# Summing the conditioning over partitions by TensorE transposes and ScalarE accumulating copies in a fused FP32 hybrid layer

## The chip, the cores and the metric

One Trainium2 chip, one core of it. The metric is the device time of the kernel in microseconds (us); the times given are medians over repeated runs. A trace of one profiled execution stands beside them. Engines are named as the trace names them: PE is TensorE's matmul, PEld its weight load, DVE is VectorE, ACT is ScalarE, POOL is GpSimd, SP is the queue that issues the DMAs.

## The reference, cut to what matters

```python
cond = jax.nn.silu(c)                                # (1, 2048)
mod = cond @ w_mod[l] + b_mod[l]                     # w_mod: (2048, 6*2048)
sh1, sc1, gt1, sh2, sc2, gt2 = jnp.split(mod, 6, axis=-1)
u = rms_norm(h, norm1_g[l]) * (1.0 + sc1) + sh1      # h: (1, 256, 2048)
aq, ak, av, rq, rf, ri, rg, ga, gr = split_columns(u @ w_in[l])
...
h = h + gt1 * (merged @ w_o[l])
u = rms_norm(h, norm2_g[l]) * (1.0 + sc2) + sh2
ffn = (jax.nn.silu(u @ w_ffn_gate[l]) * (u @ w_ffn_up[l])) @ w_ffn_down[l]
h = h + gt2 * ffn
return rms_norm(h, final_g)
```

All of it is FP32; the sequence has 256 rows, the model width is 2048. The conditioning vector `mod` decides shift (`sh`) and scale (`sc`) of both norms, so no product with `w_in` can start before the shift and scale of its rows of `u` are known.

## The kernel before, in words

**Products.** Every weight tile `w` (four k-blocks of 128 rows by 512 columns, one DMA) is cast by ACT to a rounded high part `wh` (L240), and DVE forms the low part `wl` = `w` - `wh` (L242), two k-blocks per instruction. `products` (L245) then issues three matmuls per k-block and half of the sequence: `wh` with `uH` (L250), `wl` with `uH` (L251) and `wh` with `uL` (L252), all into one accumulator `acc` per half. `wh` and `wl` live in pools of four buffers each: a fifth cast waits until PE has finished with the oldest.

**Chunks.** The columns of `w_in` for the first seven outputs are worked in 14 column groups, and the k-blocks in four chunks (3, 4, 5 and 4 blocks, `chunk_cols` and `group`): all 14 groups of chunk 0, then all 14 of chunk 1, and so on, the sums kept in SBUF tiles `part`. Between chunks 0 and 1 PE goes from products with rows 0 to 2 of `uH`, `uL` straight to products with rows 3 to 6.

**Conditioning.** `mod_cols` computes shift and scale of some k-blocks. DVE accumulates `cond`-weighted rows of `w_mod` tiles `wm` into two tiles `modc` (one for shift, one for scale; L403 starts, L407 adds), where each partition holds the sum over its own rows. What is left is a sum over the 128 partitions, and a change of layout: the result must have one column per k-block, channels on partitions. `col_sum` (L333) does both by one FP32 matmul per 128 columns with a column of ones as the moving operand: its output is a [128, 1] column of the PSUM tile `pmc`. DVE then adds the bias (L426, L427) and forms `(1 + sc) * g` (L428). For the first norm `modulated` (L378) follows for every k-block: ACT computes `u` = `xT` times scale plus shift (L373) and its high part `uH` (L383), DVE the low part `uL` (L384).

**Order of the work.** `mod_cols` is a generator. While chunk `ci` runs, `step` advances the one of chunk `ci + 1` after each weight tile; `chunk_cols` sets the pace so that it is through shortly before the chunk ends (`AHEAD` = 1.15), and `drain` runs what is left. `GAP1`, the number of steps between sums and their use, is 0 here. Three later calls (L-numbers of the profile: sums at 749, 854 and 916 us) make the second norm's conditioning while `w_o` and the first FFN tiles are worked: 16, 8 and 8 column sums. Beside those, chunk 0 has 6 sums, chunk 1 has 8, chunk 2 has 10 and chunk 3 has 8. A scheduler then puts the instructions of all engines into queues, one per engine, each of which the engine works strictly in order.

Of the kernel before, what the change touches and what calls it, by code (L numbers as in the profile page):

```python
# [8 lines left out]
F32 = mybir.dt.float32  # L9
# [3 lines left out]
AF = mybir.ActivationFunctionType  # L13
# [5 lines left out]
P = 128  # L19
D = 2048  # L20
S = 256
KT = D // P
# [29 lines left out]
def block_kernel(  # L52
# [7 lines left out]
    nc = tc.nc  # L60
    x, out = x[0], out[0]
# [4 lines left out]
    small = ctx.enter_context(tc.tile_pool(name="small", bufs=4))  # L66
# [11 lines left out]
    def bank(name):  # L78
        return ps.tile([P, 512], F32, tag="ps", name=name)

    def tmpt(name, n=512, dt=F32):
        return tmp.tile([P, n], dt, tag=f"t{n}", name=name, bufs={512: NT, 256: 2}[n])
# [7 lines left out]
    ident = const.tile([P, P], F32, name="ident")  # L90
# [137 lines left out]
    def load_mod(k0, nk, n0, ncol, own):  # L228

        if own:  # L230
            dst = wpool.tile([P, nk, ncol], F32, tag="wm", name="wm", bufs=NM)
        else:
            dst = bigt("wm0")[:, :nk * ncol].rearrange("p (k n) -> p k n", n=ncol)
        return load(w_mod, k0, nk, n0, ncol, dst)
# [98 lines left out]
    def col_sum(p, j0, a, n):  # L333
        for j in range(n):
            mm(p[:, j0 + j:j0 + j + 1], a[:, j * P:(j + 1) * P], ones[:, 0:1], start=True, stop=True)  # L335
# [4 lines left out]
    junk = const.tile([P, NG], F32, name="junk")  # L340
# [37 lines left out]
    def modulated(src, k, H, L):  # L378

        u = tmpt("u", S)  # L380
        scale_shift(UACT, u, src, k)
        h = H(k, slice(0, S))
        nc.scalar.copy(out=h, in_=u)  # L383
        nc.vector.tensor_sub(out=L(k, slice(0, S)), in0=u, in1=h.bitcast(F32))  # L384

    def mod_loads(nk):
        wid = nk * P
        kk = min(KT, 1024 // wid)
        return [(q, min(kk, KT - q)) for q in range(0, KT, kk)]

    def mod_cols(k0, nk, chunk, gcol, src, H, L, after=None, room=0, lag=0):

        wid = nk * P
        a = [tmp.tile([P, 1024], F32, tag="modc", name=f"modc{ci}", bufs=2) for ci in range(2)]
        waiting = []

        def sums(q, kk, ci, w):
            for j in range(kk):  # L400
                s1, d = cond[:, q + j:q + j + 1], a[ci][:, :wid]
                if q + j == 0:
                    first = nc.vector.tensor_scalar_mul(out=d, in0=w[:, j], scalar1=s1)  # L403
                    if after is not None:
                        tc.add_manual_dep(first.ins, after.ins.name, NOSYNC, reason="the norm goes first")
                else:
                    nc.vector.scalar_tensor_tensor(out=d, in0=w[:, j], scalar=s1, in1=d, op0=ALU.mult, op1=ALU.add)  # L407

        for q, kk in mod_loads(nk):
            for ci in range(2):  # L410
                waiting.append((q, kk, ci, load_mod(q, kk, (chunk + ci) * D + k0 * P, wid, q >= room)))
                if ci == 0:
                    yield
            while len(waiting) > (lag if q < room else 0):
                sums(*waiting.pop(0))
            yield
        for w in waiting:
            sums(*w)
        p = bank("pmc")
        for ci in range(2):  # L420
            col_sum(p, ci * nk, a[ci], nk)
        for _ in range(GAP if chunk else GAP1):
            yield
        ks = slice(k0, k0 + nk)
        bc = [bcols[:, (chunk + ci) * KT + k0:(chunk + ci) * KT + k0 + nk] for ci in range(2)]
        nc.vector.tensor_add(out=sh_col[:, ks], in0=p[:, 0:nk], in1=bc[0])  # L426
        nc.vector.tensor_add(out=sc_col[:, ks], in0=p[:, nk:2 * nk], in1=bc[1])  # L427
        nc.vector.scalar_tensor_tensor(out=sc_col[:, ks], in0=sc_col[:, ks], scalar=1.0, in1=gcol[:, ks], op0=ALU.add, op1=ALU.mult)  # L428
        if src is not None:
            for k in range(k0, k0 + nk):  # L430
                modulated(src(k, slice(0, S)), k, H, L)
# [31 lines left out]
    def mods1(ci):  # L463
        k0, nk = kchunks[ci]
        return mod_cols(k0, nk, 0, g1c, xTv, uH, uL, room=(KT, KT // 2, 0, 0)[ci], lag=(0, 4, 0, 0)[ci])
# [253 lines left out]

    cond_side.append(mod_rows("gt1", 2))  # L720
    cond_side.append(mod_cols(0, KA, 3, g2c, None, None, None))
    pace["cond"] = PACE2
    side.append(attention(0))
# [117 lines left out]
    for k0, nk in KREST:  # L841
        cond_side.append(mod_cols(k0, nk, 3, g2c, x2Tv, u2H, u2L, last_norm2[-1] if PIN else None))
        pace["cond"] += AHEAD * 2 * len(mod_loads(nk)) / nsteps
# [14 lines left out]
    for part_n, ng in enumerate((6, 5)):  # L858
        fH, fL = [None] * ng, [None] * ng
        for g in range(ng):  # L860
# [3 lines left out]
            for t in range(2):  # L864
                if early:
                    a = fpart[2 * g][:, t]
                    nc.vector.tensor_add(out=a, in0=pg[t], in1=a)
                    nc.scalar.activation(a, a, AF.Silu)
                else:
                    a = tmpt("sl")  # L870
# [62 lines left out]
```

## Time and profile before

| | |
|---|---|
| median of 3 runs | 1547.67 us (1547.43 to 1552.2) |
| profiled execution, its own time | 1543.71 us |
| its span in the trace | 1541.5 us |
| granted clock | 0.998 |
| busy: PE, DVE, ACT | 97%, 71%, 48% |
| chain of waits: PE, DVE, DMA, ACT | 89%, 5%, 3%, 2% |

"Busy" is the share of the span in which an engine had an instruction under way; a matmul's duration overlaps the next one's, so start-to-start distances, not durations, tell what a matmul costs. The chain of waits goes back from the last instruction, at each step to what released it. A row of the timeline has the start, the duration, the engine, the line, output <- inputs, shapes and count, and in brackets how long the engine had been idle and who ended it.

### The profile page before, as it was taken

Reading aid. Unit: us, or ns where it says so; the run is one execution under the profiler, and the core shown is the slowest. Engines: PE = TensorE matmul, PEld = TensorE weight load, DVE = VectorE, ACT = ScalarE, POOL = GpSimd, SP = SyncE. Lnnn points to the kernel's source line nnn. Section 1 sums busy time; section 2 is a strip of 40 time slices with the busy share of each in tenths; the row PEclk is TensorE's granted clock in tenths of the full one; section 3 lists DMA queues with packets and bytes.
Section 4 is the critical chain, followed back from the end, with each engine's and each line's share of the span. In section 5 each row is a group of like instructions: output and inputs, shape, how many; then the busy total and the mean of one; then the engine's idle time right before and its main releaser. Section 6 shows DMA issues by size and latency. Waiting matters only on the chain.

```text
span 1541.5 us, 18297 instructions
## 1 busy us (share of the span) xinstructions
PE 1495.4 (97%) x6931; PEld 1233.7 (80%) x6931; DVE 1101.4 (71%) x1439; ACT 732.4 (48%) x1015; POOL 10.5 (1%) x40
## 2 busy tenths in 40 slices
PE   3999999999999999999989999999999999999997
PEld 2788888888878778888878888888888888888885
DVE  5789997788877688987578778879555555544555
ACT  5563433524567764444464554444333444444443
POOL 1000000000000000000000000000000000000000
PEclk9999999999999999999999999999999999999999
DMA  9899998444764389899549988868555655556552
GB/s 312 306 327 320 314 322 273 165 137 150 253 239 150 110 306 337 319 333 333 194 156 352 329 316 286 296 222 304 199 196 196 196 180 191 187 187 219 190 194 103
DMA packets 175987, 373.67 MB, mean 242 GB/s; under 512 B 8430, under 2 KB 12695, under 8 KB 175899
## 3 DMA queue, kind: packets, MB, share of 16 engines
q1 hardware_dynamic: 174776, 371.77, 69.9%
q8 instruction: 54, 0.88, 0.2%
q10 hardware_dynamic: 1122, 0.74, 0.2%
q14 instruction: 35, 0.28, 0.0%
HBM read 370.38 MB, written 2.10 MB: 242 GB/s over the span
## 4 chain that ended last, share of the span: by engine, by line
PE 89%; DVE 5%; DMA 3%; ACT 2%; issue 1%; SPq 0%; DVEq 0%; ACTq 0%
PE acc L250 27%; PE acc L251 27%; PE acc L252 27%; PE ptr L504 2%; DMA wm<-in_w_mod_dram 2%; DVE wl L242 2%; PE pl L589 2%; DVE modc L407 1%; PE pmc L335 1%; DMA w<-in_w_in_dram 1%; ACT junk L343 1%; PE psc L652 0%; PE prow L330 0%; PE pav L683 0%; DMA rows<-in_gnorm_g_dram 0%
## 5 line engine op out<-in xcount | busy, mean ns | idle before, releaser
L240 ACT CAST wh<-w 128x1024 fp32r<-128x1024 f32 (+1 forms) x518 | 529.7, 1030 | 673.9 <-PE acc L252 575.5
L242 DVE TENSOR_TENSOR wl<-w,wh 128x1024 fp32r<-128x1024 f32 (+1 forms) x518 | 613.9, 1193 | 324.3 <-ACT wh L240 323.1
L250 PE MATMUL acc<-wh,uH 128*128 128x512 f32 x704 | 277.7, 394 | 2.4 <-ACT uH L383 2.4
L251 PE MATMUL acc<-wl,uH 128*128 128x512 f32 x704 | 276.7, 393 | 0.4 <-DVE wl L242 0.4
L251 PE MATMUL acc<-wl,u2H 128*128 128x512 f32 x704 | 274.4, 390 | 2.8 <-DVE wl L242 2.8
L250 PE MATMUL acc<-wh,u2H 128*128 128x512 f32 x704 | 275.4, 391 | 1.6 <-ACT u2H L794 1.6
L252 PE MATMUL acc<-wh,uL 128*128 128x512 f32 x704 | 276.4, 393 | 0.0
L252 PE MATMUL acc<-wh,u2L 128*128 128x512 f32 x704 | 275.0, 391 | 0.0
L407 DVE SCALAR_TENSOR_TENSOR modc<-wm,cond,modc 128x512 f32<-128x512 f32 (+3 forms) x210 | 166.8, 822 | 18.7 <-DMA wm<-in_w_mod_dram 17.9
L251 PEld LDWEIGHTS acc<-wl,u2H 128*128 128x128 f32 x704 | 132.2, 188 | 30.9 <-DVE wl L242 3.6
L250 PEld LDWEIGHTS acc<-wh,uH 128*128 128x128 f32 x704 | 133.0, 189 | 29.0 <-ACT uH L383 2.5
L251 PEld LDWEIGHTS acc<-wl,uH 128*128 128x128 f32 x704 | 132.8, 189 | 29.0 <-issue 1.2
L252 PEld LDWEIGHTS acc<-wh,uL 128*128 128x128 f32 x704 | 132.8, 189 | 28.2 <-issue 0.6
L250 PEld LDWEIGHTS acc<-wh,u2H 128*128 128x128 f32 x704 | 132.2, 188 | 28.9 <-ACT u2H L794 1.9
L252 PEld LDWEIGHTS acc<-wh,u2L 128*128 128x128 f32 x704 | 132.2, 188 | 27.4 <-DVE u2L L795 0.2
L251 PE MATMUL acc<-wl,fH 128*128 128x512 f32 x352 | 137.4, 390 | 0.0
L252 PE MATMUL acc<-wh,fL 128*128 128x512 f32 x352 | 137.1, 390 | 0.0
L250 PE MATMUL acc<-wh,fH 128*128 128x512 f32 x352 | 137.0, 389 | 0.0
L320 DVE SCALAR_TENSOR_TENSOR gt<-wm,cond,gt 128x1024 f32<-128x1024 f32 x64 | 81.7, 1277 | 7.4 <-DMA wm<-in_w_mod_dram 7.0
L251 PEld LDWEIGHTS acc<-wl,fH 128*128 128x128 f32 x352 | 66.1, 188 | 13.9 <-issue 0.2
L252 PEld LDWEIGHTS acc<-wh,fL 128*128 128x128 f32 x352 | 66.1, 188 | 13.8 <-issue 0.2
L250 PEld LDWEIGHTS acc<-wh,fH 128*128 128x128 f32 x352 | 66.1, 188 | 13.7
(250 smaller groups left out, 1217.6 us busy)
## 6 DMA issues: line engine op xcount, KB each, us to landing
wm<-in_w_mod_dram SPq DMA_DIRECT2D x160, 512.0 KB, 6.0
w<-in_w_in_dram SPq DMA_DIRECT2D x74, 1024.0 KB, 5.5
w<-in_w_ffn_gate_dram SPq DMA_DIRECT2D x44, 1024.0 KB, 5.2
w<-in_w_ffn_up_dram SPq DMA_DIRECT2D x44, 1024.0 KB, 7.9
w<-in_w_ffn_down_dram SPq DMA_DIRECT2D x44, 1024.0 KB, 5.1
w<-in_w_o_dram SPq DMA_DIRECT2D x16, 1024.0 KB, 6.6
w<-in_w_in_dram SPq DMA_DIRECT2D x14, 768.0 KB, 6.4
wm<-in_w_mod_dram SPq DMA_DIRECT2D x32, 320.0 KB, 5.0
```

The source lines that it names most:

```text
L240: nc.scalar.copy(out=wh, in_=src)
L242: nc.vector.tensor_sub(out=wl, in0=src, in1=wh.bitcast(F32))
L250: mm(po[t], aH(k, ts), h, start=first, stop=False)
L251: mm(po[t], aH(k, ts), lo, start=False, stop=False)
L252: mm(po[t], aL(k, ts), h, start=False, stop=last)
L320: nc.vector.scalar_tensor_tensor(out=a[i], in0=w[:, 0], scalar=cond[:, k:k + 1], in1=a[i], op0=ALU.mult, op1=ALU.add)
L335: mm(p[:, j0 + j:j0 + j + 1], a[:, j * P:(j + 1) * P], ones[:, 0:1], start=True, stop=True)
L343: return nc.scalar.activation(junk[:, :src.shape[-1]], src, AF.Square, accum_out=dst)
L407: nc.vector.scalar_tensor_tensor(out=d, in0=w[:, j], scalar=s1, in1=d, op0=ALU.mult, op1=ALU.add)
L504: nc.tensor.transpose(out=p[:, j * P:(j + 1) * P], in_=src[:, j * P:(j + 1) * P], identity=ident)
L589: mm(p[:, (4 * b + j) * 64:(4 * b + j + 1) * 64], kb[:, j, b * P:(b + 1) * P], qb[:, j, b, :, 1, :], start=True, stop=True)
```

## The change

For every call except that of chunk 0 (`room < KT`), the sums over partitions are made another way. Up to four 128-column blocks of `modc` are transposed on PE into a PSUM tile `pmt`; then ACT copies each transposed block to a scratch tile `junk` with an accumulating output, which adds up its 128 columns, that is the 128 partitions of before, into one column of the SBUF tile `mcs`. After every batch of four but the last the generator yields, so that a later batch is issued one step later. Bias, scale, `u`, `uH` and `uL` follow as before. 58 of the 64 column sums change. Line numbers from L432 on rise by 13; L426 to L428 of before are L439 to L441 after, and L426 and L428 are now the transpose and the summing copy.

```diff
@@ mod_cols
         for w in waiting:
             sums(*w)
-        p = bank("pmc")
-        for ci in range(2):
-            col_sum(p, ci * nk, a[ci], nk)
+        if room < KT:
+            p = small.tile([P, 2 * nk], F32, tag="mcs", name="mcs", bufs=2)
+            for j0 in range(0, 2 * nk, 4):
+                n = min(4, 2 * nk - j0)
+                pt = bank("pmt")
+                for j in range(n):
+                    ci, k = divmod(j0 + j, nk)
+                    nc.tensor.transpose(out=pt[:, j * P:(j + 1) * P], in_=a[ci][:, k * P:(k + 1) * P], identity=ident)
+                for j in range(n):
+                    nc.scalar.activation(junk[:, :P], pt[:, j * P:(j + 1) * P], AF.Copy, accum_out=p[:, j0 + j:j0 + j + 1])
+                if j0 + n < 2 * nk:
+                    yield
+        else:
+            p = bank("pmc")
+            for ci in range(2):
+                col_sum(p, ci * nk, a[ci], nk)
         for _ in range(GAP if chunk else GAP1):
             yield
```

The order of the queues moves with it. On PE before, at the end of chunk 0: the 8 sums `pmc`, then the last column group of the chunk (18 products, `acc_867` and `acc_868`), then the first products of chunk 1 (`acc_928`). `uH_295` and `uL_299` hold k-blocks 0 to 3, `uH_296` and `uL_300` blocks 4 to 7.

```order
L335 MATMUL pmc<-ones,modc_355 128x1 x4
L335 MATMUL pmc<-ones,modc_356 128x1 x4
L250 MATMUL acc_867<-wh,uH_295 128x512
L251 MATMUL acc_867<-wl,uH_295 128x512
...
L250 MATMUL acc_868<-wh,uH_295 128x512
L251 MATMUL acc_868<-wl,uH_295 128x512
L252 MATMUL acc_868<-wh,uL_299 128x512
L250 MATMUL acc_928<-wh,uH_295 128x512
```

The same place on PE after the change: the last group is `acc_849` and `acc_850`, and chunk 1 begins with `acc_938`.

```order
L426 MATMUL pmt<-ident,modc_355 128x128 x4
L250 MATMUL acc_849<-wh,uH_295 128x512
L251 MATMUL acc_849<-wl,uH_295 128x512
...
L250 MATMUL acc_850<-wh,uH_295 128x512
L251 MATMUL acc_850<-wl,uH_295 128x512
L252 MATMUL acc_850<-wh,uL_299 128x512
L426 MATMUL pmt<-ident,modc_356 128x128 x4
L250 MATMUL acc_938<-wh,uH_295 128x512
L251 MATMUL acc_938<-wl,uH_295 128x512
L252 MATMUL acc_938<-wh,uL_299 128x512
```

All sums stood one column group ahead of chunk 1; now half of them, the scale's, stand directly ahead of it. At the ends of chunk 1 (last 2 of 10 sums) and chunk 2 (last 4 of 8) the same happens, with 24 and 30 products in the group that has been passed.

ACT after the change, at that place: `wh_1006` is the second cast of the weight tile `w_988`, `pmt_879` the last transposes, `u_891` the first modulated block of chunk 1.

```order
L240 CAST wh_990<-w_988 128x1024
L428 ACTIVATE junk_99,mcs_836<-pmt_879 128x128
L240 CAST wh_1006<-w_988 128x1024
L428 ACTIVATE junk_99,mcs_836<-pmt_879 128x128 x3
L373 ACTIVATE u_891<-xT0_227,sh_col_101,sc_col_100 128x256
L373 ACTIVATE u_895<-xT1_228,sh_col_101,sc_col_100 128x256
L383 CAST uH0_295<-u_891 128x256
L383 CAST uH1_296<-u_895 128x256
```

A cast has come between the sums of the last batch, and all of them stand ahead of `u` and `uH`, which ACT before began with directly.

DVE after the change, at that place: `wl_1008` belongs to `wh_1006`; `wm_1026` and `wm_1066` are tiles of `w_mod` for chunk 2's conditioning.

```order
L242 TENSOR_TENSOR wl_992<-w_988,wh_990 128x1024
L242 TENSOR_TENSOR wl_1008<-w_988,wh_1006 128x1024
L440 TENSOR_TENSOR sc_col_100<-mcs_836,bcols_94 128x4
L407 SCALAR_TENSOR_TENSOR modc0_974<-wm_1026,cond_90,modc0_974 128x640
L441 SCALAR_TENSOR_TENSOR sc_col_100<-sc_col_100,cols_93 128x4
L407 SCALAR_TENSOR_TENSOR modc1_975<-wm_1066,cond_90,modc1_975 128x640
L384 TENSOR_TENSOR uL0_299<-u_891,uH0_295 128x256
L384 TENSOR_TENSOR uL1_300<-u_895,uH1_296 128x256
```

The scale has moved behind the subtraction `wl_1008`, and one accumulation of chunk 2 each stands ahead of its second half and of the first `uL`.

## Rows read from the trace of the kernel before

**Rows 1.** The page: span, busy time of each engine; chain that ended last, by line.

```profile
PE 1495.4 (97%) x6931; PEld 1233.7 (80%) x6931; DVE 1101.4 (71%) x1439; ACT 732.4 (48%) x1015; POOL 10.5 (1%) x40
...
PE acc L250 27%; PE acc L251 27%; PE acc L252 27%; PE ptr L504 2%; DMA wm<-in_w_mod_dram 2%; DVE wl L242 2%; PE pl L589 2%; DVE modc L407 1%; PE pmc L335 1%; DMA w<-in_w_in_dram 1%; ACT junk L343 1%; PE psc L652 0%; PE prow L330 0%; PE pav L683 0%; DMA rows<-in_gnorm_g_dram 0%
```

**Rows 2.** Waits of PE from 40 to 300 us: us in total, times, longest.

```profile
PE acc L250 <- ACT uH L383: 2.4, 1, 2.4
PE acc L251 <- DVE wl L242: 0.4, 1, 0.4
```

**Rows 3.** Timeline of PE at the end of chunk 0.

```profile
95.07 1.84 PE L335 MATMUL pmc<-ones,modc 128*128 128x1 f32 x16
96.78 0.49 PE L250 MATMUL acc<-wh,uH 128*128 128x512 f32 x1
...
101.00 0.39 PE L250 MATMUL acc<-wh,uH 128*128 128x512 f32 x1
```

**Rows 4.** Timeline of PE at the end of chunk 1.

```profile
172.49 2.29 PE L335 MATMUL pmc<-ones,modc 128*128 128x1 f32 x20
174.64 0.49 PE L250 MATMUL acc<-wh,uH 128*128 128x512 f32 x1
...
180.23 0.39 PE L250 MATMUL acc<-wh,uH 128*128 128x512 f32 x1
```

**Rows 5.** Timeline of PE at the end of chunk 2.

```profile
268.63 1.84 PE L335 MATMUL pmc<-ones,modc 128*128 128x1 f32 x16
270.33 0.49 PE L250 MATMUL acc<-wh,uH 128*128 128x512 f32 x1
...
277.27 0.39 PE L250 MATMUL acc<-wh,uH 128*128 128x512 f32 x1
```

**Rows 6.** Timeline of PE at a batch of 16 transposes of FP32 128x128 blocks.

```profile
293.60 1.91 PE L504 MATMUL ptr<-ident,part 128*128 128x128 f32 x16
295.26 0.47 PE L250 MATMUL acc<-wh,uH 128*128 128x512 f32 x1
```

**Rows 7.** Timeline of ACT at four accumulating activations of 128x128 from PSUM.

```profile
549.26 0.28 ACT L343 ACTIVATE junk<-pav 128x128 f32<-128x128 f32 x1 [1.33 <-PE pav L683]
...
550.73 1.04 ACT L240 CAST wh<-w 128x1024 fp32r<-128x1024 f32 x1
```

**Rows 8.** Timeline of all engines from chunk 0's sums to its first products.

```profile
36.20 0.99 PE L335 MATMUL pmc<-ones,modc 128*128 128x1 f32 x4
...
37.37 0.68 DVE L242 TENSOR_TENSOR wl<-w,wh 128x512 fp32r<-128x512 f32 x1
...
38.16 1.09 ACT L373 ACTIVATE u<-xT,sh_col,sc_col 128x256 f32<-128x256 f32 x2 [2.21 <-DVE sc_col L428]
...
39.16 0.70 ACT L383 CAST uH<-u 128x256 fp32r<-128x256 f32 x2
...
39.60 0.79 PE L250 MATMUL acc<-wh,uH 128*128 128x512 f32 x1 [2.41 <-ACT uH L383]
```

**Rows 9.** The page, costliest groups: busy us, mean ns of one, idle before.

```profile
L240 ACT CAST wh<-w 128x1024 fp32r<-128x1024 f32 (+1 forms) x518 | 529.7, 1030 | 673.9 <-PE acc L252 575.5
L242 DVE TENSOR_TENSOR wl<-w,wh 128x1024 fp32r<-128x1024 f32 (+1 forms) x518 | 613.9, 1193 | 324.3 <-ACT wh L240 323.1
```

**Rows 10.** Timeline of DVE at the end of chunk 0.

```profile
101.99 0.89 DVE L407 SCALAR_TENSOR_TENSOR modc<-wm,cond,modc 128x640 f32<-128x640 f32 x1 [1.22 <-DMA wm<-in_w_mod_dram]
```

**Rows 11.** The page, DMA issues: KB each, median us from issue to landing.

```profile
wm<-in_w_mod_dram SPq DMA_DIRECT2D x160, 512.0 KB, 6.0
```

**Rows 12.** Windows, chunk 1: PE, PEld, DVE, ACT, POOL busy, clock, DMA share, GB/s.

```profile
95.00:172.00 77.00, 76.59 (x346) 63.22 (x345) 72.98 (x91) 32.76 (x40) 0.00 (x0) 1.00 0.93 324
```

**Rows 13.** Timeline of PE, the twelfth product of chunk 0.

```profile
44.46 0.43 PE L252 MATMUL acc<-wh,uL 128*128 128x512 f32 x1
```

**Rows 14.** Timeline of PE after a wait in the first FFN group.

```profile
788.10 0.50 PE L250 MATMUL acc<-wh,u2H 128*128 128x512 f32 x1 [1.62 <-ACT u2H L794]
788.43 0.40 PE L251 MATMUL acc<-wl,u2H 128*128 128x512 f32 x1
```

## Prediction

> **What bounds the kernel now.** I begin with the page: PE is busy 97% of the span, and the three product lines make 81% of the chain, the column sums 1% [rows 1]. So only two things count: time that PE spends on other work than products, and time that PE stands. Next I look at PE's waits in chunks 0 to 2: in 260 us PE waited once 2.4 us (start of chunk 0) and once 0.4 us [rows 2], so it crosses all three chunk ends without standing. PE's timeline there tells why: after the sums come 18, 24 and 30 products, 4.22, 5.59 and 6.94 us [rows 3 to 5], before the first product of the next chunk; this is the cover under which scale, `u`, `uH` and `uL` are made. What that chain takes uncovered is seen at chunk 0: `pmc` ends at 37.19 (36.20 + 0.99), the first product starts at 39.60, so **2.4 us** [rows 8]. A product takes 0.23 us (6.94 / 30).
>
> **What PE saves.** 8 sums took 96.78 - 95.07 = 1.71 us, 10 took 2.15, 8 took 1.70 [rows 3 to 5]: 0.214 us each. 16 transposes took 295.26 - 293.60 = 1.66 us, 0.104 each [rows 6]. Each batch also costs the product behind it about 0.09 us (0.23 becomes 0.33: 4.22 us for 18 products instead of 4.1) [rows 3], and there are more batches: two for one at chunk ends 0, 1 and 2, three for one at the 16 sums beside `w_o`, two for one in one of the two FFN calls. So PE saves 0.8 (8 sums), 1.0 (10), 0.8 (8), 1.6 (16: 1.76 - 0.18), 0.8 (8) and 0.9 (8, one batch): **5.9 us**, 0.4%.
>
> A row of a transpose lasts far longer than 0.104 us (1.91 for the merged row of 16 ends 0.25 us after the next product began [rows 6]), because rows overlap; I take start to start. The Trainium skill ("TensorE: Matmul & The Clock Gate", Part 4: PE-mode transpose) gives about 275 ns for a 128x128 transpose inside a kernel. By that figure, an estimate, 58 transposes would take 16.0 us against 12.4 for the sums, and PE would lose 3.6 us where I book a gain of 5.9; the 0.104 us measured here contradicts it as a cost in a stream.
>
> **What ACT and DVE pay.** Four accumulating activations of this size took 550.73 - 549.26 = 1.5 us [rows 7], nearly 0.4 each; 58 add 22 us to ACT, which is 48% busy [rows 1]. By itself that costs nothing: the cover is ACT's idle time ahead of its casts (674 us, ended mostly by PE freeing a `wh` buffer [rows 9]). DVE's three small instructions are the same.
>
> **What the order takes away.** The extra step puts the last batch behind the column group that was the cover. On PE it stands directly ahead of the first product of the next chunk, which needs `uH`, which needs `u`, the whole scale, and so this last batch. PE's queue is in order: it must stand from the end of these transposes until the chain is through. The least this can cost: the 2.4 us above plus the sums of the last batch on ACT (1.5, 0.8, 1.5), less what PE saved there (0.8, 1.0, 0.8): 3.1 + 2.2 + 3.1 = 8.4. The queues of ACT and DVE add work that stands ahead of these steps.
>
> *End of chunk 0.* PE reaches the last batch at 95.07 + 0.42 + 0.09 + 4.1 = 99.7 and ends it at 100.1. On ACT a cast stands among the four sums, on a buffer that PE frees with the group's last product: one sum to 100.5, cast 1.0 [rows 9], three sums 1.1, to 102.6. DVE does the `wl` of that cast in the meantime (1.2 [rows 9], to 102.7), half of the scale, one accumulation of chunk 2 (0.9 [rows 10]), the other half: 103.8. Then two `u` (1.1) and the first `uH` (0.35) [rows 8]: 105.2 to 105.5, where before the same product started at 101.00 [rows 3]. `uL` is behind another accumulation, whose `w_mod` tile may be late (here one came 1.22 late already [rows 10]). I take a loss of **5.0**, between 4 and 7.
>
> *End of chunk 1.* PE ends its two transposes at 172.49 + 0.83 + 0.09 + 5.5 + 0.21 = 179.1. A 512-wide cast (0.5, half of a row of [rows 9]) and two sums (0.8) follow to 180.4, scale with one 512-wide start of chunk 3's sums to 181.0, `u` and `uH` to 182.5; before, that product ran at 180.23 [rows 4]: 2.3 us at least. But the first `uL` stands behind three accumulations of chunk 3, whose 512 KB tiles take 6.0 us to land [rows 11] and two of which can be issued only at about 178 to 179, when DVE has given their buffers back: 184 to 186, up to 7 lost with the accumulations behind them. I take **4.5**, the middle.
>
> *End of chunk 2.* PE ends the batch at 268.63 + 0.42 + 0.09 + 6.8 + 0.42 = 276.4. One cast on a buffer freed at 276.0 lasts to 277.0, four sums to 278.5, scale 0.3, two `u` and `uH` 1.5: 280.3 to 280.7, against 277.27 [rows 5]. No `w_mod` tile stands in between. **3.3**, between 2.8 and 3.8.
>
> *The later calls.* Beside `w_o` the sums are used long after (the second norm), and in the FFN parts 18 or more products after; I found no new wait of PE there. Gain 1.6 + 0.8 + 0.9 = **3.3**. (The gains at the chunk ends are already in the arrival times above.)
>
> **The sum.** 5.0 + 4.5 + 3.3 - 3.3 = **+9.5 us**; low 8.4 - 3.3 = +5.1; high 7 + 7 + 3.8 - 3.3 = +14.5. On the profiled execution that is 1543.7 + 9.5 = 1553.2. The median of the runs lies 4.0 above that execution (1547.67), so the median after should be **1557.2 us**, +0.6%.
>
> **Rivals.**
>
> *Faster: the stands are paid back.* If PE's pace through chunks 1 to 3 were set by loads or DVE, both would run on while PE stands, and the later groups would go quicker by as much; only the 5.9 us would be left: 1541.8. For it: DVE was busy 72.98 of 77 us in chunk 1, DMA at 0.93 [rows 12]. Against it: PE was busy 76.59 of those 77, so there is at most 0.4 us to win back there. It decides if PE's waits in chunks 1 to 3 of before summed to the new stands, some 15 us (12.8 and the 2.6 saved ahead of them); they sum to 0.4 [rows 2]. Chance 0.06.
>
> *No change.* The chain at each end is quicker than I have it (`u` and `uH` of single blocks instead of pairs, a cast done early because PE stands later), about 2 us less each than taken: +3.5, 1551. For it: the waits in [rows 8] hold a 0.7 us subtraction by DVE that need not be there. Against: even the least cost is 8.4 - 3.3. Chance 0.12.
>
> *Late `w_mod` tiles.* If accumulations wait for their tiles ahead of scale or `uL`, ends 0 and 1 cost 7 each: 1562. It decides when a tile is issued under 6 us before its turn. Chance 0.12.
>
> *A slower TensorE clock after the stands.* The first eleven products of chunk 0, after a stretch in which PE stood often, took 44.46 - 39.60 = 4.86 us, 0.43 to 0.44 each, where 11 x 0.23 = 2.5 is usual [rows 8, 13]: 0.43 is what 512 columns take at 1.2 GHz, half of the full clock. So one fall costs 2.3 us. After a wait of 1.62 us in the FFN the products were at full pace at once [rows 14]; waits of 3 to 5 us inside a stream are not in this trace. With a fall at one to three ends: +11.8 to +16.4, 1559.5 to 1564.1. Chance 0.20. The Trainium skill (same page, "Why this matters for your kernels") speaks against long idle gaps between matmul bursts, since the clock drops; the half pace at the start of chunk 0 agrees, and no row shows it for gaps of this length.
>
> *Transposes dear.* If transposes of `modc` did not overlap, each could cost what the last of the 16 lasts, 1.91 - 15 x 0.104 = 0.35 us: 58 x 0.25 = 14 us more, 1571. The start-to-start time in [rows 6] speaks against it. Chance 0.02.
>
> **How the numbers follow.** The forecast itself has 0.48. A measurement of this kernel can tell about 0.3%, 4.6 us, from no change. Faster by more: only the first rival, 0.06. Within: the second, 0.12. Slower: the rest, 0.82. The range leaves out the first rival, half of the second and the last, about 0.14: its low end is 1550, its high end the clock's worst case, 1564.
>
> **What would show it.** In the new profile PE's waits must have new rows: the first products of chunks 1 to 3 on ACT `uH` (or third products on DVE `uL`), some 5 to 6, 3.5 to 7 and 4 us long; 16 transposes in about 1.7 us beside `w_o`, where 16 sums at 0.214 took 3.4; ACT busy some 22 us more; PE busy about 6 us less. If the waits at the ends sum to under 10 us, or PE's gain is under 4, a step is wrong. If the products after a stand come 0.43 us apart, the clock rival holds.

## The result: slower, and by more than forecast

| | before | after |
|---|---|---|
| median, us | 1548.78 (4 runs, 1547.43 to 1552.2) | 1567.12 (4 runs, 1561.37 to 1569.07) |
| ratio to before | | 1.0111, 95% interval 1.0092 to 1.013 |
| span in the trace | 1541.5 | 1565.0 |
| granted clock | 0.998 | 0.987 |

The sign was right; the size was not: +18.3 us where +9.5 was forecast, and 1567 lies 3 us above the top of the range. The two granted clocks don't cover the same stretch: the record of the trace before begins only at 44.5 us, that of the trace after has 0.50 from 31 to 44 us already. The stands below make up about half of the difference. First the page after, busy time and the chain by line, to be held against [rows 1]:

```profile
PE 1495.4 (96%) x6873; PEld 1229.8 (79%) x6873; DVE 1102.3 (70%) x1439; ACT 753.5 (48%) x1131; POOL 10.5 (1%) x40
...
PE acc L252 25%; PE acc L251 25%; PE acc L250 25%; DMA wm<-in_w_mod_dram 6%; DVE wl L242 2%; PE ptr L517 2%; PE pl L602 2%; DVE modc L407 2%; DVE part L472 1%; ACT junk L343 0%; PE psc L665 0%; ACT wh L240 0%; DVE gt L320 0%; DMA lv<-in_lambda_q_dram 0%; DMA rows<-in_lb_logits_dram 0%
```

ACT is busy 21 us more (22 were booked). The column sums have left the chain, the products hold 75% of it instead of 81%, and `w_mod` loads 6% instead of 2%. PE's busy time is the same to a tenth, although 58 transposes are cheaper than 58 sums: something else has grown longer. PE's waits over the whole run (us in total, times, longest) say where it stands, against one wait of 2.4 us on `uH` before [rows 2]:

```profile
PE acc L250 <- ACT uH L383: 18.7, 4, 6.2
...
PE acc L250 <- ACT wh L240: 2.3, 2, 1.2
...
PE acc L250 <- DVE part L472: 0.9, 1, 0.9
```

Three of the four waits on `uH` are new, 16.3 us, one at each chunk end. PE's timeline at the end of chunk 0, which answers to [rows 3]:

```profile
99.76 0.60 PE L426 MATMUL pmt<-ident,modc 128*128 128x128 f32 x4
106.55 0.79 PE L250 MATMUL acc<-wh,uH 128*128 128x512 f32 x1 [6.20 <-ACT uH L383]
...
108.56 0.80 PE L252 MATMUL acc<-wh,uL 128*128 128x512 f32 x1 [0.78 <-DVE uL L384]
109.15 0.63 PE L250 MATMUL acc<-wh,uH 128*128 128x512 f32 x1
109.58 0.63 PE L251 MATMUL acc<-wl,uH 128*128 128x512 f32 x1
...
112.78 0.39 PE L250 MATMUL acc<-wh,uH 128*128 128x512 f32 x1
113.00 0.39 PE L251 MATMUL acc<-wl,uH 128*128 128x512 f32 x1
```

The transposes end at 100.2 and the first product of chunk 1 starts at 106.55, 5.5 us later than at 101.00 before. Then products come 0.43 us apart (109.15 to 109.58), and only from 112.5 on 0.22 to 0.24. What PE waited for stands on ACT and DVE, in the same stretch:

```profile
100.72 1.04 ACT L240 CAST wh<-w 128x1024 fp32r<-128x1024 f32 x1
...
102.45 0.28 ACT L428 ACTIVATE junk<-pmt 128x128 f32<-128x128 f32 x1
...
101.78 2.35 DVE L242 TENSOR_TENSOR wl<-w,wh 128x1024 fp32r<-128x1024 f32 x2
104.06 0.15 DVE L440 TENSOR_TENSOR sc_col<-mcs,bcols 128x4 f32<-128x4 f32 x1
104.13 0.88 DVE L407 SCALAR_TENSOR_TENSOR modc<-wm,cond,modc 128x640 f32<-128x640 f32 x1
104.92 0.15 DVE L441 SCALAR_TENSOR_TENSOR sc_col<-sc_col,cols 128x4 f32<-128x4 f32 x1
105.11 1.09 ACT L373 ACTIVATE u<-xT,sh_col,sc_col 128x256 f32<-128x256 f32 x2 [2.29 <-DVE sc_col L441]
106.11 0.69 ACT L383 CAST uH<-u 128x256 fp32r<-128x256 f32 x2
...
107.28 0.88 DVE L407 SCALAR_TENSOR_TENSOR modc<-wm,cond,modc 128x640 f32<-128x640 f32 x1 [2.21 <-DMA wm<-in_w_mod_dram]
108.08 0.75 DVE L384 TENSOR_TENSOR uL<-u,uH 128x256 fp32r<-128x256 f32 x2
```

It is the chain of the prediction with one piece more: the cast among the sums, the last sum from 102.45 on, the scale behind two `wl` in a row on DVE (one was booked) and an accumulation, `u`, `uH`; and `uL` behind an accumulation whose tile came late. PE at the ends of chunks 1 and 2, against [rows 4, 5]:

```profile
191.27 0.38 PE L426 MATMUL pmt<-ident,modc 128*128 128x128 f32 x2
197.73 0.79 PE L250 MATMUL acc<-wh,uH 128*128 128x512 f32 x1 [6.08 <-ACT uH L383]
...
295.24 0.60 PE L426 MATMUL pmt<-ident,modc 128*128 128x128 f32 x4
299.81 0.50 PE L250 MATMUL acc<-wh,uH 128*128 128x512 f32 x1 [3.98 <-ACT uH L383]
...
300.93 0.63 PE L250 MATMUL acc<-wh,uH 128*128 128x512 f32 x1
301.36 0.63 PE L251 MATMUL acc<-wl,uH 128*128 128x512 f32 x1
```

The end of chunk 2 is the chain of the prediction again. At the end of chunk 1 something else ends the wait. ACT is through with its sums at 192.8 and then stands 3.50 us for the scale, because DVE, busy without a pause, reaches it only at 195.63, behind two accumulations, two `wl` and two additions to `part`:

```profile
193.84 1.28 DVE L472 TENSOR_TENSOR part<-acc,part 128x512 f32<-128x512 f32 x2
...
195.63 0.15 DVE L440 TENSOR_TENSOR sc_col<-mcs,bcols 128x5 f32<-128x5 f32 x1
...
196.29 1.09 ACT L373 ACTIVATE u<-xT,sh_col,sc_col 128x256 f32<-128x256 f32 x2 [3.50 <-DVE sc_col L441]
```

The windows show the slow products too (columns as in [rows 12]; the last three are granted clock, DMA share and GB/s):

```profile
106.50:112.20 5.70, 4.86 (x11) 3.37 (x12) 3.82 (x7) 2.96 (x7) 0.00 (x0) 0.50 0.96 334
...
197.70:201.00 3.30, 3.27 (x8) 2.39 (x9) 3.30 (x6) 1.82 (x5) 0.00 (x0) 0.50 0.96 346
...
300.00:304.00 4.00, 4.00 (x11) 3.11 (x11) 1.31 (x4) 1.76 (x5) 0.00 (x0) 0.57 0.55 212
```

A granted clock of 0.50 is the lower level, 1.2 GHz: after each of the three stands PE worked at half pace. That is what filled PE's busy time up again.

**Ledger.** The n-th product of one trace is the n-th of the other, so the lag of the changed kernel can be read at every product. I take the last group of chunk 0 ahead of the first transposes as zero:

| what | lag added, us | booked |
|---|---|---|
| first product of chunk 1 | 5.45 | 5.0 |
| next 12 products: late `uL` 0.78, half pace 2.7 | 3.46 | 0 |
| waits within chunk 1 for weight tiles and an accumulator | 3.4 | 0 |
| first product of chunk 2 | 5.06 | 4.5 |
| half pace after it | 1.8 | 0 |
| first product of chunk 3 | 3.2 | 3.3 |
| half pace after it | 1.8 | 0 |
| later calls (beside `w_o`, first FFN parts) | -3.6 | -3.3 |

That is +20.6. The rest of the 23.5 us between the two spans lies mostly between the end of chunk 2 and `w_o`, where the lag of the traces below moves by up to 5.4 us whatever the kernel; I leave it unexplained. The traced execution before (1543.71) was also a quick one, 5 us under the median, so the traces lie further apart than the medians (18.3).

### The profile page after: what moved, and what is told of

Its sections match the earlier page's. It is cut to its first block, busy times and chain, and to the rows that moved or that the text cites. A ratio compares the mean times of both kernels' runs of the same rounds, so it can differ in the third digit from the quotient of the medians.

```text
span 1565.0 us, 18306 instructions
## 1 busy us (share of the span) xinstructions
PE 1495.4 (96%) x6873; PEld 1229.8 (79%) x6873; DVE 1102.3 (70%) x1439; ACT 753.5 (48%) x1131; POOL 10.5 (1%) x40
## 4 chain that ended last, share of the span: by engine, by line
PE 80%; DVE 8%; DMA 7%; ACT 2%; issue 2%; ACTq 0%; SPq 0%; DVEq 0%
PE acc L252 25%; PE acc L251 25%; PE acc L250 25%; DMA wm<-in_w_mod_dram 6%; DVE wl L242 2%; PE ptr L517 2%; PE pl L602 2%; DVE modc L407 2%; DVE part L472 1%; ACT junk L343 0%; PE psc L665 0%; ACT wh L240 0%; DVE gt L320 0%; DMA lv<-in_lambda_q_dram 0%; DMA rows<-in_lb_logits_dram 0%
```

## Experiments

Three theories stood against each other. **Place:** the extra step takes the last batch behind the group that covered the chain. **Queue:** transposes and copies on ACT make the chain long wherever it stands. **Clock:** standing makes TensorE slow afterwards. Times of each set are compared with runs of the kernel before on the same chip (1548.7, 1550.9 and 1549.2 us for the three sets below). "Lag" is the ledger's, to the middle of chunk 3's first group; it is 24.2 for the changed kernel.

### No extra step (e1_one_place)

```diff
-                if j0 + n < 2 * nk:
-                    yield
```

> The change without its extra step: all transposes and summing copies of a call are issued in one place, ahead of the last column group of the chunk. Theory (the place of the last batch costs the time): the cover of 18, 24 and 30 products is back. The chain is longer than with the column sums by 8 or 10 copies of 0.4 us (3.2 to 4.0 us and 2.4 us against 4.2, 5.6 and 6.9 us of cover), so PE may still stand 1 to 3 us at the first two chunk ends, not at the third, and too short for the clock to fall; with 5.9 us less PE work the time is 2 to 5 us under the kernel before, 1544 to 1547. Rival (the new way of summing itself, transposes and 58 copies on ACT, costs the time wherever it stands): stands of 4 to 6 us stay, 1560 or more.

Measured: 1549.35 us against 1548.72, ratio 1.0004 (0.9991 to 1.0016). So without the two lines nearly the whole loss is gone, but PE's saving doesn't show. Its waits in chunks 0 to 2, and ACT at the first end:

```profile
PE acc L250 <- ACT part L468: 5.3, 1, 5.3
PE acc L250 <- ACT uH L383: 3.2, 1, 3.2
```

```profile
104.58 0.69 ACT L383 CAST uH<-u 128x256 fp32r<-128x256 f32 x2
105.18 2.02 ACT L468 COPY part<-acc 128x512 f32<-128x512 f32 x4
```

The third end has no stand, as expected, the second has one of 3.2, the first one of 5.3, more than expected, and not on the chain: the eight copies hold ACT up, `u` and `uH` come late, and the four copies of finished accumulators to `part` queue behind them, so that PE has no accumulator for its first product. ACT worked from 97.4 to 108 with one pause of 0.5 us. Both stands were followed by half pace (granted clock 0.50 from 105.7 to 109.2 and from 187.7 to 191.1), which had not been expected, and the time lies above the 1544 to 1547 of the theory. Place is the larger part; the queue is a second one.

### The extra step alone (e2_split_sums)

```diff
         p = bank("pmc")
-        for ci in range(2):
-            col_sum(p, ci * nk, a[ci], nk)
+        for j0 in range(0, 2 * nk, 4):
+            n = min(4, 2 * nk - j0)
+            for j in range(j0, j0 + n):
+                ci, k = divmod(j, nk)
+                col_sum(p, j, a[ci][:, k * P:], 1)
+            if room < KT and j0 + n < 2 * nk:
+                yield
```

> The kernel before with its column sums by ones, but issued in batches of four with the extra step between, as the change does: no transposes, no copies on ACT. Theory (place): PE stands at the three chunk ends for about 4.5 to 6, 4 to 6 and 2.5 us, the clock falls after the longer ones, and nothing is saved on PE: 1563 to 1570, as slow as the changed kernel or slower. Rival (the new way of summing costs the time): the column sums need no ACT, so 1547 to 1551 as before.

Measured: 1556.78 us, ratio 1.0055 (1.003 to 1.008). PE waits for `uH` four times, 10.0 us in all:

```profile
PE acc L250 <- ACT uH L383: 10.0, 4, 2.7
```

The place alone makes stands (2.5, 2.7 and 2.4 us at the three ends, beside the old 2.4), but the size was missed: they are about as long as the chain of [rows 8], where I had expected more casts and accumulations ahead of it. In this kernel's queues most of those stand elsewhere. Place alone costs 8 us, the new sums without the step cost nothing net, both together 18: more than their sum. The copies lengthen a chain that has lost its cover, and the late tiles of the ledger came with neither alone; no run here says how much is due to which.

### The later calls alone (e3_late_only)

```diff
-        if room < KT:
+        if chunk:
```

> The change only in the three later calls (second norm), the column sums by ones at the chunk ends as before. Theory: the later sums have time to spare, so only PE's saving is left: 3.3 us by the prediction's terms, 3.7 us by the ledger of the two traces, 1544 to 1546 where before has 1548. Rival (copies on ACT delay casts, PE waits for them): 0 or slower, 1548 to 1552.

Measured: 1542.92 us, ratio 0.9964 (0.995 to 0.9978), faster than before by 5.6 us of 1548.72, the interval reaching from 3.4 to 7.7. The 3.6 of the ledger lies at its edge; what the gain beyond it comes from isn't shown. PE has no stand in chunks 0 to 2 but the old one and 0.8 us for an accumulator:

```profile
PE acc L250 <- ACT uH L383: 2.4, 1, 2.4
PE acc L250 <- ACT part L470: 0.8, 1, 0.8
```

Where nobody waits for the sums, transposes are the better way. The saving on PE may not be all of it: in two of the three traces that have the 16 column sums beside `w_o` in one batch, the clock fell behind that batch (last section).

### PE kept busy during the stands (e4_filler, f4_long_filler)

```diff
+        if room < KT and not chunk:
+            pf = bank("pfill")
+            for _ in range(FILL):
+                mm(pf[:, :P], ones, ident, start=True, stop=True)
         for _ in range(GAP if chunk else GAP1):
             yield
```

> The change with 20 matmuls of ones by the identity (FP32, 128 columns, a result nobody reads) behind the last transposes of the three chunk ends, so that PE works some 4.3 us of each stand. Theory (PE's standing makes the clock fall): products after the ends come 0.23 us apart at once, granted clock 1.00 in those stretches, first products at the same time as in the changed kernel or 0.3 us later; 2.4 + 1.6 + 1.7 = 5 to 6 us under the changed kernel. Rival (the slow products have another cause: fresh operands, transfers): 0.43 us apart all the same, time as the changed kernel or up to 1 us slower.

Measured: 1559.87 us, ratio 1.0068 (1.0045 to 1.009), 0.43% or 6.7 us under the changed kernel, though the filler at the third end outlasts the stand. The clock is not all of that. The lag is 17.9 against 24.2, and 4.1 us of the difference lie within chunk 1, where this kernel has no late weight tiles. The ends of chunks 1 and 2 together cost 3.6 us less, the first end 1.4 more. The expectation of 5 to 6 counted the clock alone, so that it came near is luck. Windows behind the first and the second end:

```profile
108.00:112.00 4.00, 4.00 (x10) 3.13 (x11) 2.53 (x5) 2.34 (x6) 0.00 (x0) 0.50 0.95 327
...
194.00:198.00 4.00, 4.00 (x19) 3.29 (x18) 2.44 (x6) 3.21 (x7) 0.00 (x0) 1.00 0.91 311
```

At the second and third end the clock stayed at 1.00. At the first, where 20 matmuls left PE idle for 2.7 us and for 0.7 more, it fell all the same. So the filler was made longer:

```diff
-            for _ in range(FILL):
+            for _ in range(FILL if room == 0 else 30):
```

The text below says the ends of chunks 0 and 1; this edit makes it 30 at the end of chunk 0 only, and leaves 20 at the other two, where 20 had been enough.

> As the kernel with 20 filler matmuls, but 30 (6.4 us) at the ends of chunks 0 and 1, where 20 left PE idle for 2.7 and 0.7 us at the first end. Theory (idle time and not the interruption makes the clock fall): granted clock 1.00 after all three ends, the first products 0.23 us apart, 2 to 3 us less from the first end to its 36th product than with 20, less up to 0.6 us by which the filler may outlast the stand: 0 to 3 us under that kernel. Rival: half pace at the first end all the same.

Measured: 1559.59 us, ratio 1.0065 (1.0044 to 1.0086). The window behind the first end:

```profile
106.00:110.00 4.00, 2.92 (x14) 2.11 (x13) 3.14 (x6) 2.24 (x6) 0.00 (x0) 1.00 0.92 319
```

Now all three ends keep 1.00, with the first product no earlier than in the changed kernel. From the first end to the middle of the next group the lag falls from 10.3 (20 matmuls) to 7.1 us; of that the timed runs show little (0.3 us, inside the intervals). The clock theory holds at these places: with PE kept busy during the stand the same products run at full pace, so neither the transposes nor the fresh operands make them slow. The Trainium skill ("TensorE: Matmul & The Clock Gate", Why this matters for your kernels) warns of the same, gaps between matmul bursts; these windows agree.

### One end at a time (e5_first_end, e6_other_ends)

```diff
-        if room < KT:
+        if 0 < room < KT and not chunk:
```

> The change at the end of chunk 0 only; column sums by ones everywhere else. Theory (each end pays for itself): stand and slow clock there as in the changed kernel, 8.9 us by the ledger of the traces. Whether the 3.4 us that the changed kernel lost in chunk 1 to late weight tiles follow from this stand is open: if they do, 1559 to 1562, if not, 1556 to 1558, where before has 1548.7.

```diff
-        if room < KT:
+        if room == 0 and not chunk:
```

> The change at the ends of chunks 1 and 2 only. Theory (each end pays for itself): 6.6 and 5.2 us as in the ledger, 1559 to 1562. If the late weight tiles in chunk 1 come from the stand at the end of chunk 0, PE doesn't wait within chunk 1 here; if they come from how the chunk-2 conditioning is made, it does, some 3 us.

Measured against 1550.94: the first end alone 1562.71, ratio 1.008 (1.0056 to 1.0103); the other two alone 1560.88, ratio 1.0065 (1.0048 to 1.0081). By the ratios that is 12.4 and 10.1 us; with the 5.6 of the later calls taken off, 16.9, near the 18.3 of all together. That the ends only add up is not quite so: the end of chunk 1 stands 4.24 us here, where it stood 6.08 behind the first end's stand. Both traces also hold falls of the clock behind column sums, worth 5.7 and 3.6 us, which are not of these ends (last section). The loss within chunk 1 goes with the first end. PE's waits from the clock's recovery to the end of chunk 1, first the first-end kernel, then (whole of chunk 1) the other:

```profile
PE acc L250 <- ACT wh L240: 2.3, 2, 1.1
PE acc L250 <- DVE part L472: 1.0, 1, 1.0
```

```profile
PE acc L251 <- DVE wl L242: 0.5, 1, 0.5
```

### Sums on DVE (e7_vector_sums, e8_vector_one_place)

```diff
-                for j in range(n):
-                    nc.scalar.activation(junk[:, :P], pt[:, j * P:(j + 1) * P], AF.Copy, accum_out=p[:, j0 + j:j0 + j + 1])
+                nc.vector.reduce_sum(out=p[:, j0:j0 + n], in_=pt[:, :n * P].rearrange("p (j q) -> p j q", q=P), axis=AX.X)
```

> The changed kernel with the sums over the transposed blocks on DVE, one reduction per batch of up to four blocks, in place of four accumulating copies on ACT; the places and the extra step stay. Theory (the stands beyond the 2.4 us chain come from ACT's queue: copies, and casts between them): stands of 2.5 to 4 us as with the split column sums, little or no slow clock, PE's saving of 6 us against that kernel's 1556.8: 1550 to 1554. Rival (it is the place alone): stands of 4 to 6 us, 1562 or more.

Measured: 1560.09 us against 1550.94, ratio 1.0061 (1.0043 to 1.0079); relative to before that is 0.5% under the changed kernel. The stands at the three ends are 3.9, 3.6 and 3.9 us, the upper edge of what was expected; each was followed by half pace, which I had not expected, and that is why the time is over 1554. ACT's copies and casts account for some 2.3 us of the first stand, and the place for the rest. The 2.4 us at the second end are not ACT's: with the copies on ACT and four `w_mod` buffers (below) it stands 3.68. Late weight tiles in chunk 1 are missing here too, which is part of the gain.

Without the extra step:

> The same sums on DVE, and no extra step: all batches of a call in one place ahead of the last column group. Theory: chain about 1.5 us longer than with column sums, inside the cover of 4.2 to 6.9 us, so at most 1 us of stand at the first end, and PE's saving of 6 us shows: 1542 to 1545. Rival (ACT's copies of partial sums and casts are late at the first end anyhow, as with the one-place kernel): PE waits 3 to 5 us there for an accumulator, 1546 to 1549.

Measured: 1552.67 us, ratio 1.0013 (1.0002 to 1.0024). The waits in chunks 0 to 2:

```profile
PE acc L250 <- ACT uH L383: 7.6, 2, 5.2
PE acc L250 <- ACT part L467: 4.6, 1, 4.6
```

The rival's wait for an accumulator is there at the first end, and the second end stands 5.2 us, which neither had: scale came late there on DVE. Half pace followed both, and the time lies above both ranges. A lighter chain in the same place isn't enough; how the queues are ordered around it decides.

### Sums much earlier (f1_vector_ahead)

```diff
-AHEAD = 1.15
+AHEAD = 1.3
```

(on top of the kernel just above)

> Transposes, sums on DVE, no extra step, and the conditioning's pace during chunks 0 to 2 raised from 1.15 to 1.3, which puts the transposes 50 or more products (11 us) ahead of the next chunk. Theory (the stands come from a chain longer than its cover): no stand at any chunk end, PE's saving of 6 us shows: 5 to 7 us under the kernel before of the same chip. Rival (the w_mod tiles asked for 13% sooner collide with weight loads, which fill 0.93 of the DMA time in chunk 1): PE waits there for weight tiles, 3 us or more, so 0 to 3 us under before.

Measured: 1549.51 us against 1549.22, ratio 1.0 (0.9984 to 1.0016). No stand on `uH` at any chunk end, only the old 2.4 at the start, but:

```profile
PE acc L251 <- DVE wl L242: 3.3, 6, 0.7
...
PE acc L250 <- ACT wh L240: 1.1, 1, 1.1
```

PE now waits 4.4 us for weight tiles and their low parts within the chunks (0.4 before), as the rival has it. The faster pace holds for the later calls too: beside the first FFN tiles, at 848 us, PE waits 1.42 and 0.42 us more, half pace follows (granted clock 0.50 from 850.1 to 853.5), and the lag grows by 4.8 us. The cover is back, and what it costs is as much as PE saves.

### Four buffers for w_mod tiles (f3_wm4)

```diff
-BIG = 27
-NW, NM, NH, SK = 3, 3, 4, 2
+BIG = 26
+NW, NM, NH, SK = 3, 4, 4, 2
```

> The changed kernel with four buffers for w_mod tiles in place of three (and 26 large buffers in place of 27 to make room). Theory for the late weight tiles in chunk 1 (w_mod tiles are issued only when DVE gives a buffer back, and the loads behind them in the same queue wait too): DVE's 12 us of waits for w_mod tiles in chunk 1 shrink to under 4, PE's 3.3 us there vanish, 3 to 5 us under the changed kernel. Rival (the stand's own backlog of casts and sums): PE waits in chunk 1 as in the changed kernel, time as there.

Measured: 1560.88 us, ratio 1.0073 (1.0053 to 1.0093), 0.38% or 5.9 us under the changed kernel. DVE's waits from 110 to 185 us, the changed kernel first, then this one:

```profile
DVE modc L407 <- DMA wm<-in_w_mod_dram: 9.7, 7, 1.9
DVE wl L242 <- ACT wh L240: 3.0, 1, 3.0
```

```profile
DVE wl L242 <- ACT wh L240: 8.9, 7, 3.6
```

No wait for `w_mod` tiles is left in that stretch, and PE doesn't wait at all within chunk 1, where the changed kernel's lag grew by 3.4 us. DVE is then no longer behind at the end of chunk 1, which stands 3.68 us instead of 6.08 and costs 2.7 instead of 5.06. These two make up the gain. So a fourth buffer removes the late tiles, as the theory has it: a tile is issued only when DVE gives one back, and weight tiles queue behind it. What sets them off isn't shown: the two kernels with filler and the one with sums on DVE have three buffers and a late first product, and no such loss.

### The best version (f2_late_and_third)

```diff
-        if room < KT:
+        if chunk or k0 == 12:
```

(with the sums on DVE and no extra step)

> Column sums by ones at the ends of chunks 0 and 1; transposes and sums on DVE, in one place, at the end of chunk 2 (the longest cover, 6.9 us) and in the three later calls. Theory: no stand anywhere, and PE saves 0.9 us at that end and 3.7 us later: 4 to 7 us under before. Rival (what the later-calls-only kernel gained over 3.7 us was chance, and DVE's reductions cost more than ACT's copies): 2 to 4 us under before.

Measured: 1543.9 us against 1549.22, ratio 0.9963 (0.995 to 0.9975). Faster than before and than the change, but not to be told from the later calls alone (0.9964). Against the theory PE still waits 0.8 us for an accumulator and 0.7 us for a `wl`, and the clock fell once, from 178.6 to 182.0 us, behind the 10 column sums of the end of chunk 1.

## Why the forecast was right and wrong

- **What bounds the kernel** held: what the ledger explains is PE standing or PE slow, at the places the order of the queues named, but for the waits within chunk 1.
- **PE's saving** held where nobody waits: 8 transposes of the end of chunk 1 took 0.79 us start to start (0.83 booked), and the later calls gave 3.6 us where 3.3 were booked. The Trainium skill's 275 ns per transpose ("TensorE: Matmul & The Clock Gate", Part 4: PE-mode transpose), which the page gives beside a bf16 figure, would, as an estimate, have made them a loss; here one cost 0.1 us in a stream.

```profile
184.94 1.03 PE L426 MATMUL pmt<-ident,modc 128*128 128x128 f32 x8
185.73 0.48 PE L250 MATMUL acc<-wh,uH 128*128 128x512 f32 x1
```

- **What the order takes away** held at the first and the third end: 5.45 and 3.2 against 5.0 and 3.3; the late `uL` was seen, 0.78 us. At the end of chunk 1, 5.06 against 4.5 is luck. The 4.5 was the middle between 2.3 for the chain and 7 for a first `uL` behind late tiles; the wait was on `uH`, and its length came from DVE, whose queue brought the scale 3.50 us late. With four `w_mod` buffers the same place costs 2.7, near the 2.3 of the chain alone.
- **Wrong: "A slower TensorE clock after the stands"** stood as a rival with a chance of 0.20, beside the forecast. The sum put it at nothing. It came at all three ends and cost 2.7 + 1.8 + 1.8 = 6.3 us, near what was priced (2.3 each, 6.9). The price was read rightly as half pace: the trace before has no clock record ahead of 44.5 us, but the one after shows 0.50 up to 44.2, where its chunk 0 picks up pace too. [Rows 14] had been read as evidence against it, a wait of 1.62 us without a fall; stands of 4 to 6 us are another thing, and three long stands were what I had just forecast. The fall belonged into the sum.
- **Wrong: "Late `w_mod` tiles"** was looked for only ahead of scale and `uL`. It cost 0.8 there, 3.4 within chunk 1, where no step had looked, and by the run with four buffers some 2.4 more at the end of chunk 1. The loads run at 0.93 of their time in chunk 1 [rows 12], so little can be caught up; but why it happens in this kernel and not behind the filled stands stays open.
- **Wrong: the range.** Its top took one rival at a time. They are no alternatives: all three came in one kernel, each behind a stand. 9.5 + 6.3 + 3.4 = 19.2 on 1547.7 is 1566.9, close to the 1567.1 measured. That it fits to the microsecond is luck too: the terms are of two traces that lie 23.5 us apart, the medians 18.3.
- **"Faster: the stands are paid back"** has no support: apart from the places where transposes stand for sums, the lag fell by no more than 0.7 us anywhere in chunks 1 to 3.

## What to carry to other kernels

Before moving a reduction, look at which instruction of the bounding engine stands behind its last part in the queue: a step that takes half of a small job behind the block of work that hid it can cost the whole chain, whatever the job itself saves. Count what follows a stand of TensorE, too (half pace, a load queue that stood as well), as part of the stand and not as another case. And change only the calls whose result nobody awaits: here that alone was worth 0.36%, where the same edit made everywhere cost 1.1%.

## What was not expected of the hardware

- The clock fell with PE never idle. In the kernel changed at the first end only, 16 column sums beside `w_o` took 3.93 us and half pace followed for 13 products; the kernel changed at the other two ends shows the same (4.36 us), the kernel before, with 3.48 us, doesn't. Behind the 10 sums at the end of chunk 1 it fell in two traces (first end only, best version) and not in two others (before, later calls only). No trace shows it behind the transposes that replace the 16. PE and the window behind it:

```profile
770.91 4.06 PE L335 MATMUL pmc<-ones,modc 128*128 128x1 f32 x32
774.84 0.77 PE L250 MATMUL acc<-wh,mH 128*128 128x512 f32 x1
```

```profile
774.80:780.80 6.00, 6.00 (x15) 4.74 (x16) 1.54 (x4) 0.46 (x1) 0.00 (x0) 0.50 0.50 163
```

- Half pace came behind shorter stands as well. In the kernel with split column sums, stands of 2.51 and 2.67 us were followed by half pace, one of 2.41 us was not (granted clock 1.00 from 287 to 290). Each stood right behind column sums, so what the stand alone does isn't shown. The first of the three:

```profile
103.00:106.00 3.00, 3.00 (x11) 2.35 (x10) 3.00 (x6) 3.00 (x7) 0.00 (x0) 0.67 0.96 318
```

- The fall can come late: after the 3.98 us stand the first two products still ran at 0.34 and 0.35 us and the half pace set in behind them, while after the 6.2 us stand the first was slow already.
- Ordinary FP32 matmuls nobody reads, put into a stand, kept the clock at 1.00 behind it: 30 at the first end and 20 at the other two. How much time that alone gives isn't shown, since these kernels also had no late tiles; the first of them came out 0.43% under the changed kernel.
